# A four-layer trunk on one core: first gate tiles plain, operand sums of x moved, weight splits off GpSimd

## The chip, the cores and the metric

One core of one Trainium2 chip runs the whole program in one launch. The metric is the device time of one execution in microseconds (us), given as the median of several runs.

TensorE (PE in the profile) multiplies, VectorE (DVE), ScalarE (ACT) and GpSimd (POOL) do everything elementwise, and SyncE (SP) issues most DMAs. PEld is TensorE's weight load, listed apart from the matmuls.

## The reference, cut to what matters

The trunk has four residual layers over x, 512 tokens by 1024 features, in float32: pooling, gated convolution, latent attention, pooling. Each normalises x, multiplies by one input projection that yields the branch and a gate of width 2048, and ends in an output projection.

```
def rms_norm(x, g):  y = x * rsqrt(mean(x * x) + eps);  return y * g

def pool_mixer(xn, w_in, w_grp, scale, w_out):
    u, z = split(xn @ w_in, 2)                 # 2048 columns each
    for g, w in enumerate((2, 4, 8, 16)):      # groups of 512 columns
        pooled[g] = trailing_mean(u[g], w) - u[g]
        mixed[g] = pooled[g] @ w_grp[g]
    return (mixed * scale * silu(z)) @ w_out

def mla_mixer(...):                            # 16 heads
    q, k, v = low-rank latents @ up-projections;  p = softmax(q k^T + rotary part)
    return (p v * silu(z)) @ w_out
```

## The kernel before

**Precision.** Every operand of a matmul is split into a high part and the rest: ACT copies a tile to `fp32r` (h), DVE subtracts (l = value minus h). A product is then three matmuls: h by h, h by l, l by h (`mm3`, L256). The weights arrive in float32 and are split in the same way: `prepare_chunk` (L237) splits a chunk of 128x1024, ACT writing `wh` (L244) and DVE `wl` (L247). With `pool=True` both halves are done by POOL (L242, L247).

**Jobs.** The projections run as a stream of jobs (`Stream`, L184). One job is a plain tile (`Layer.tile`, L469): 24 matmuls 128x512 with one 512 KB chunk of weights; or a pair (`Layer.pair`, L484): two output tiles by seven half-width products (`seven`, L428), 84 matmuls of 256 columns. A pair needs weight blocks and their sums (`load_pair`, `prepare_pair`, L113 and L385: four loads from SP, an accumulating one from POOL, and on DVE the splits al, sl, cl, two sums, two tl) and needs the sums and differences of the halves of x (`XNorm.forms`, L350: per pair of x tiles four operations d at L362 to L365 on 128x256, two splits fh, fl). Its results E and O leave PSUM by two DVE operations (L458, L459).

**Order.** Each job has positions 0 to 7 (`now(k)`). The other engines' work is put on positions with `Steps.put`; what is put past 7 runs in later jobs. `Stream.step` (L213) loads the weights of the next two jobs, and puts the splitting of the next job's weights (`wh` on position 1, `wl` on 2) behind what already stands on the same position. Within the stream, TensorE, VectorE and ScalarE run strictly in the written order. GpSimd is not in that list. The attention heads (L1059 to L1085) are outside the stream, and there the framework's planner sets the order.

**The first layer.** Jobs in order: the first two u tiles with x still arriving (`first_two`), u02, u03, u10 to u13, the gate pairs z00 and z01, the mixes m00 and m01, the pairs z10 and z11, and so on (`ORDER`, L583). The normalising factor R comes from the statistics of x and is known after u11 (`at=(4, 6)`); until then six u tiles wait in PSUM. Then each gets (`post_u`, L595) a multiplication by R (L579, read from PSUM), adds with shifted copies on POOL (L608: one for group 0, two for group 1), a mean on DVE (L615, L616, L617), and a split (L620 on ACT, L623 on DVE); mean, high and low stand 12, 14 and 16 positions after the multiplication. The six start one position apart (`gap` 1). The forms of x for kk = 0 to 3 begin on positions 0, 8, 16 and 24 after `first_two`, one set in each of u02, u03, u10 and u11.

**Between layers.** `out_part` (L522) adds each output tile to x and puts the next layer's `xn.add(m)`, whose forms are delayed by `wait=8 * (KD - 2 - m + m // 2)`: set kk = 0 in the last job of the output projection, the others in the next layer's first three jobs. The convolution has four plain tiles before its first pair, the attention layer six.

**The attention heads.** Weight chunks are split by `wchunk(..., pool=True)` in `values`, `qrope` and `stage_a`; POOL also scales the softmax (L1021). From head 10, `split_y(nc.gpsimd)` takes the low part of two gated outputs per head (L1055). Transposes of p (L1034) wait for the scaling.

Of the kernel before, what the change touches and what calls it, by code (L numbers as in the profile page):

```python
# [9 lines left out]
F32 = mybir.dt.float32  # L10
# [54 lines left out]
def trunk_kernel(ctx: ExitStack, tc: tile.TileContext, a):  # L65
# [9 lines left out]
    def nm(s):  # L75
        cnt[0] += 1
        return f"{s}_{cnt[0]}"
# [86 lines left out]
    class Steps:  # L164
# [3 lines left out]
        def __init__(self, at=()):  # L168
            self.at = dict(at)

        def put(self, at, by=0):
            for pos, fns in at.items():
                self.at.setdefault(pos + by, []).extend(fns)

        def __call__(self, pos):
            while True:
# [7 lines left out]
    class Stream:  # L184
# [28 lines left out]
        def step(self):  # L213
            j = self.at
            self.at += 1
            self.load(j + 1)
            self.load(j + 2)
            now, self.later = self.later, Steps()
            now.put(self.prepare(j + 1), 2 if self.jobs[j][0] is PAIR and self.jobs[j + 1 :] and self.jobs[j + 1][0] is not PAIR else 0)
            self.jobs[j][2](self.ready.pop(j, None), now)  # L220
            now(7)
            left, self.later = self.later, Steps()
            self.later.put(now.at, -8)
            self.later.put(left.at)
# [297 lines left out]
    def out_part(stream, w, ys, hf, xn=None, also=(), scale=None):  # L522

        thens = []
        for m in range(KD):

            def then(o, m=m):
                if scale is not None:
                    t = ut("xs")
                    tmul(t, o, scale())  # L530
                    o = t
                nc.vector.tensor_tensor(out=xt[m], in0=o, in1=xt[m], op=ALU.add)
                if xn is not None:
                    stream.later.put(xn.add(m, wait=8 * (KD - 2 - m + m // 2)))
                if m < len(also):
                    also[m]()

            if m < 2:
                thens.append(then)
            else:  # L540
                stream.add(*half_job(w, ys, m, hf, lambda: ps("o"), 0, 8, then))
            if m == 1:

                open_ = []

# [12 lines left out]

                for q in range(2):
                    stream.add(CHUNK, w[q, hf], lambda wl, now, q=q: part(wl, now, q))  # L560
# [17 lines left out]
    def tmul(dst, src, R):  # L578
        nc.vector.tensor_tensor(out=dst, in0=src, in1=R, op=ALU.mult)  # L579
# [6 lines left out]
    def pool_layer(stream, j, xn, half, mid=None, at=(1, 3), pre=None):  # L586

        wu, wz, wg = a[f"pool_u{j}"], a[f"pool_z{j}"], a[f"pool_grp{j}"]
        ys = [[], []]
        ly = Layer(xn, at, 3 if pre is None else 1)  # L590
        u_, z_, m_ = {}, {}, {}
        for g, w in enumerate(WINDOWS):
            pooled, szs = [], []

            def post_u(t, sign, g=g, w=w, pooled=pooled):  # L595
                u = up.tile([P, S + PAD], F32, tag="u", name=nm("u"))
                h, l = ut("plh", F32R), ut("pll", F32R)
                pooled.append((h, l))
                sums = []

                def mul():
                    nc.gpsimd.memset(u[:, :PAD], 0.0)
                    tmul(u[:, PAD:], t, ly.R[sign])
                    cur, d = u, 1
                    while d < w:
                        nx = up.tile([P, S + PAD], F32, tag="u", name=nm("s"))
                        lo = 2 * d - 1
                        nc.gpsimd.tensor_tensor(out=nx[:, lo:], in0=cur[:, lo:], in1=cur[:, lo - d : S + PAD - d], op=ALU.add)  # L608
                        cur, d = nx, 2 * d
                    sums.append(cur)  # L610

                def mean():
                    cur, pd = sums[0], sums[0][:, PAD:]
                    hd = sp.tile([P, PAD], F32, tag="hd", name=nm("hd"))
                    nc.vector.tensor_tensor(out=hd, in0=cur[:, PAD : 2 * PAD], in1=con[:, C_INV + PAD * g : C_INV + PAD * (g + 1)], op=ALU.mult)  # L615
                    nc.vector.scalar_tensor_tensor(out=pd, in0=cur[:, PAD:], scalar=1.0 / w, in1=u[:, PAD:], op0=ALU.mult, op1=ALU.subtract)  # L616
                    nc.vector.tensor_tensor(out=pd[:, :PAD], in0=hd, in1=u[:, PAD : 2 * PAD], op=ALU.subtract)  # L617

                def high():
                    nc.scalar.activation(h, sums[0][:, PAD:], AF.Copy)  # L620

                def low():
                    nc.vector.tensor_tensor(out=l, in0=sums[0][:, PAD:], in1=f(h), op=ALU.subtract)  # L623

                return {0: [mul], 12: [mean], 14: [high], 16: [low]}

            def post_z(t, sign, szs=szs):
                def scale():
                    tmul(t, t, ly.R[sign])

                def gate():
                    nc.scalar.activation(t, t, AF.Silu)
                    szs.append(t)

                return {0: [scale], 3: [gate]}

# [25 lines left out]
            for i in range(4):  # L662
                u_[g, i] = lambda g=g, i=i, post_u=post_u: ly.tile(stream, wu[4 * g + i], post_u)
            for i in range(2):
                z_[g, i] = lambda g=g, i=i, post_z=post_z: ly.pair(stream, wz[2 * g + i], (post_z, post_z), mid and mid(g, i))
                m_[g, i] = lambda mix=mix, i=i: mix(i)
            if g == 0 and pre is not None:
                u_[0, 0] = lambda post_u=post_u: stream.add(None, None, lambda w, now: ly.done(stream, *[(post_u, t, 1) for t in pre()]))
# [116 lines left out]
    def mla_layer(stream, xn, begin, cos_sin, nxt):  # L785
# [159 lines left out]
        krh, krl = kr  # L945

        def values(g):
            wh, wl = wchunk(wv[g], pool=True)
            for tk in range(NT):
                pv = ps("pv")  # L950
                for k in range(2):
# [6 lines left out]
                vs[g, tk] = split(pv, "v")  # L958

        def qrope(g):  # L960
            wh, wl = wchunk(wq[8 + g], 768, pool=True)
            ab = []
            for e in range(2):
                pa = ps("pa")
# [19 lines left out]

        def stage_a(h):
            if h % 2 == 0:
                hold["q"] = wchunk(wq[h // 2], 768, pool=True)
            if h % 4 == 0:
                hold["k"] = wchunk(wk[h // 4], pool=True)
            pq = ps("pq")  # L990
            mtile(pq, *hold["q"], ql, kn=3, ktot=3, stride=2 * P, off=(h % 2) * P)
            q = split(pq, "q")
# [66 lines left out]
        for h in range(H):  # L1059
# [17 lines left out]
            extra(3)  # L1077
            if h >= SPLIT_Y_FROM:
                for _ in range(2):
                    split_y(nc.gpsimd)  # L1080
            if h + 1 == H:
                nxt.begin()
                nxt.step()
# [25 lines left out]
    def first_two():  # L1109
# [30 lines left out]
            s1.later.put({m: [lambda m=m: xn0.st.add(xt[m])]})  # L1140
        s1.later.put({10: [xn0.st.close]})
        for kk in range(KK):
            s1.later.put(xn0.forms(kk), 8 * kk)
        return pre

    pool_layer(s1, 0, xn0, half, at=(4, 6), pre=first_two)
# [136 lines left out]
def _layout(i):  # L1283
# [38 lines left out]
    }  # L1322
    for j in range(2):
        out[f"pool_u{j}"] = w_in(i["pool_w_in"][j][:, :DI])
        out[f"pool_z{j}"] = w_pair(i["pool_w_in"][j][:, DI:])
        out[f"pool_grp{j}"] = i["pool_w_grp"][j].reshape(4, 4, P, 2, 2 * P).transpose(0, 3, 2, 1, 4).reshape(4, 2, P, CH)
    w = i["mla_w_in"][0]
# [28 lines left out]
```

## Time and profile before

| | us |
|---|---|
| median of 3 runs (1519.23 to 1524.7) | 1521.63 |
| the profiled execution | 1516.26 |
| its span | 1514.4 |
| TensorE busy in the span | 1455.7 (96%) |
| VectorE busy | 1096.8 (72%) |
| ScalarE busy | 677.9 (45%) |
| GpSimd busy | 324.9 (21%) |

The profile takes one execution. Of the busy times only those near the whole span bound it on their own; an engine's wait is listed with what ended it. In the rows below, a duration includes the time in which an instruction is held up after it has started.

### The profile page before, as it was taken

Reading aid. Unit: us, or ns where it says so; the run is one execution under the profiler, and the core shown is the slowest. Engines: PE = TensorE matmul, PEld = TensorE weight load, DVE = VectorE, ACT = ScalarE, POOL = GpSimd, SP = SyncE. Lnnn points to the kernel's source line nnn. Section 1 sums busy time; section 2 is a strip of 40 time slices with the busy share of each in tenths; the row PEclk is TensorE's granted clock in tenths of the full one; section 3 lists DMA queues with packets and bytes.
Section 4 is the critical chain, followed back from the end, with each engine's and each line's share of the span. In section 5 each row is a group of like instructions: output and inputs, shape, how many; then the busy total and the mean of one; then the engine's idle time right before and its main releaser. Section 6 shows DMA issues by size and latency. Waiting matters only on the chain.

```text
span 1514.4 us, 22602 instructions
## 1 busy us (share of the span) xinstructions
PE 1455.7 (96%) x8632; PEld 1281.9 (85%) x8632; DVE 1096.8 (72%) x1757; ACT 677.9 (45%) x1170; POOL 324.9 (21%) x337
## 2 busy tenths in 40 slices
PE   9799999999999999999989998999999999999997
PEld 7698797887999899999869977888888798888886
DVE  7985557659989879998778867666655487755854
ACT  5353242445555335554455644444633354323333
POOL 2502206021000000000211014355501122310602
PEclk9899999999999999999999999999999999999999
DMA  6353354325676366665236641222122434333431
GB/s 218 89 136 119 88 149 98 126 84 121 180 194 174 126 148 182 173 188 174 84 90 170 169 130 37 69 70 84 43 84 84 111 107 110 129 101 114 123 112 56
DMA packets 66012, 183.30 MB, mean 121 GB/s; under 512 B 8176, under 2 KB 8176, under 8 KB 65904
## 3 DMA queue, kind: packets, MB, share of 16 engines
q1 hardware_dynamic: 57264, 151.97, 31.2%
q0 software_dynamic: 7776, 28.32, 11.4%
q10 hardware_dynamic: 864, 1.57, 0.3%
q8 instruction: 68, 1.11, 0.3%
q14 instruction: 40, 0.33, 0.1%
HBM read 175.27 MB, written 2.10 MB: 117 GB/s over the span
## 4 chain that ended last, share of the span: by engine, by line
PE 68%; DVE 16%; DMA 4%; issue 4%; ACT 4%; POOL 2%; SPq 0%; POOLq 0%; DVEq 0%; ACTq 0%
PE o L259 6%; PE o L257 6%; PE o L258 6%; PE bx L425 5%; PE bx L419 5%; PE bx L424 5%; PE bv L419 3%; PE bv L425 3%; PE bv L424 3%; PE pt L257 3%; PE pt L258 3%; PE pt L259 3%; DMA s<-in_conv_in 2%; DVE wl L247 2%; PE po L258 2%
## 5 line engine op out<-in xcount | busy, mean ns | idle before, releaser
L247 DVE TENSOR_TENSOR wl<-wr,wh 128x1024 fp32r<-128x1024 f32 (+1 forms) x120 | 154.2, 1286 | 52.5 <-ACT wh L244 52.4
L244 ACT ACTIVATE wh<-wr 128x1024 fp32r<-128x1024 f32 (+1 forms) x120 | 125.5, 1048 | 129.9 <-PE o L258 48.2
L259 PE MATMUL o<-yh,wl 128*128 128x512 f32 x384 | 151.6, 395 | 1.9 <-DVE wl L247 1.9
L258 PE MATMUL o<-yl,wh 128*128 128x512 f32 x384 | 151.2, 394 | 0.2 <-DVE yl L656 0.2
L257 PE MATMUL o<-yh,wh 128*128 128x512 f32 x384 | 151.3, 394 | 0.1
L259 PE MATMUL pt<-xh,wl 128*128 128x512 f32 x335 | 132.1, 395 | 4.1 <-DVE wl L247 4.1
L257 PE MATMUL pt<-xh,wh 128*128 128x512 f32 x335 | 132.8, 397 | 2.1 <-ACT xh L347 1.2
L258 PE MATMUL pt<-xl,wh 128*128 128x512 f32 x335 | 132.0, 394 | 0.6 <-DVE xl L348 0.6
L120 POOL DMA_DIRECT2D s<-in_conv_in x30 | 26.0, 868 | 324.4 <-DVE O L459 154.1
L439 ACT ACTIVATE kept<-bv 128x256 f32<-128x256 f32 x54 | 20.7, 384 | 163.5 <-PE bv L425 119.1
L395 DVE TENSOR_TENSOR sl<-s,sh 128x1024 fp32r<-128x1024 f32 x54 | 66.7, 1236 | 30.5 <-ACT sh L392 26.5
L259 PEld LDWEIGHTS o<-yh,wl 128*128 128x128 f32 x384 | 72.1, 188 | 19.5 <-DVE wl L247 2.8
L258 PEld LDWEIGHTS o<-yl,wh 128*128 128x128 f32 x384 | 72.1, 188 | 17.4 <-DVE yl L656 0.5
L257 PEld LDWEIGHTS o<-yh,wh 128*128 128x128 f32 x384 | 72.1, 188 | 16.9 <-ACT yh L653 0.5
L281 POOL TENSOR_TENSOR sq<-sq,sq 128x512 f32<-128x512 f32 x25 | 40.1, 1606 | 210.8 <-ACT sq L275 210.6
L608 POOL TENSOR_TENSOR s<-u 128x527 f32<-128x527 f32 x32 | 48.0, 1501 | 164.9 <-DVE u L579 135.2
L259 PEld LDWEIGHTS pt<-xh,wl 128*128 128x128 f32 x335 | 62.9, 188 | 20.4 <-DVE wl L247 6.1
L257 PEld LDWEIGHTS pt<-xh,wh 128*128 128x128 f32 x335 | 62.9, 188 | 17.5 <-ACT xh L347 2.1
L395 DVE TENSOR_TENSOR al<-wr,ah 128x1024 fp32r<-128x1024 f32 x54 | 66.5, 1232 | 14.5 <-ACT ah L392 12.4
L258 PEld LDWEIGHTS pt<-xl,wh 128*128 128x128 f32 x335 | 62.9, 188 | 15.6 <-DVE xl L348 1.5
L439 ACT ACTIVATE kept<-bx 128x512 f32<-128x512 f32 x108 | 53.0, 490 | 45.6 <-PE bx L425 45.6
L608 POOL TENSOR_TENSOR s<-s 128x525 f32<-128x525 f32 (+2 forms) x48 | 70.0, 1458 | 12.8 <-PE pm L258 9.6
(307 smaller groups left out, 4782.9 us busy)
## 6 DMA issues: line engine op xcount, KB each, us to landing
wr<-in_conv_in SPq DMA_DIRECT2D x34, 512.0 KB, 5.6
wr<-in_pool_out SPq DMA_DIRECT2D x32, 512.0 KB, 3.3
wr<-in_pool_u SPq DMA_DIRECT2D x30, 512.0 KB, 3.5
s<-in_conv_in SPq DMA_DIRECT2D x60, 256.0 KB, 4.5
s<-in_conv_in POOLq DMA_DIRECT2D x30, 512.0 KB, 6.2
wr<-in_pool_z SPq DMA_DIRECT2D x16, 512.0 KB, 4.3
s<-in_pool_z SPq DMA_DIRECT2D x32, 256.0 KB, 3.9
s<-in_pool_z POOLq DMA_DIRECT2D x16, 512.0 KB, 6.0
```

The costliest lines, as they stand in the source:

```text
L244: nc.scalar.activation(h, raw, AF.Copy)
L247: (nc.gpsimd if pool else nc.vector).tensor_tensor(out=l, in0=raw, in1=f(h), op=ALU.subtract)
L257: nc.tensor.matmul(out, ah, bh, start=first, stop=False)
L258: nc.tensor.matmul(out, ah, bl, start=False, stop=False)
L259: nc.tensor.matmul(out, al, bh, start=False, stop=last)
L281: eng.tensor_tensor(out=self.sum, in0=self.sum, in1=sq, op=ALU.add)
L395: return lambda: nc.vector.tensor_tensor(out=l, in0=t, in1=f(h), op=ALU.subtract)
L419: i = nc.tensor.matmul(out, wh[:, c], xh, start=begin and kk == 0, stop=False, skip_group_check=True)
L424: nc.tensor.matmul(out, wh[:, c], xl, start=False, stop=False, skip_group_check=True)
L425: nc.tensor.matmul(out, wl[:, c], xh, start=False, stop=end and kk == KK - 1, skip_group_check=True)
L439: nc.scalar.activation(dst, src, AF.Copy)
L608: nc.gpsimd.tensor_tensor(out=nx[:, lo:], in0=cur[:, lo:], in1=cur[:, lo - d : S + PAD - d], op=ALU.add)
```

## The change

The first layer's z00 and z01 become two plain tiles each, with their own copy of the weights (`pool_z00`), written to fresh tiles before the gate. The waiting u tiles start six positions apart, and the forms of x begin on positions 24, 40, 56 and 72. The forms after `out_part` come one job later. The weight splits of the next job are put ahead of what stands on the same position. The chunks in the attention heads are split by ACT and DVE, and `split_y` uses DVE. The adds of `post_u` are written as a list of steps on the same position.

```
-        def put(self, at, by=0):
+        def put(self, at, by=0, first=False):
             for pos, fns in at.items():
-                self.at.setdefault(pos + by, []).extend(fns)
+                l = self.at.setdefault(pos + by, [])
+                l[:] = [*fns, *l] if first else [*l, *fns]
...
-            now.put(self.prepare(j + 1), 2 if ... else 0)
+            now.put(self.prepare(j + 1), 2 if ... else 0, first=True)
...
-                    stream.later.put(xn.add(m, wait=8 * (KD - 2 - m + m // 2)))
+                    stream.later.put(xn.add(m, wait=8 * (KD - 1 - m + m // 2)))
...
-        ly = Layer(xn, at, 3 if pre is None else 1)
+        ly = Layer(xn, at, 3 if pre is None else 6)
...
+        def two_tiles(stream, src, posts, then):
+            for q in range(2):
+                ly.tile(stream, a["pool_z00"][len(zs)], posts[q], then if q else None)
+                zs.append(q)
...
-                return {0: [mul], 12: [mean], 14: [high], 16: [low]}
+                adds = [lambda q=q: add(2**q) for q in range(g + 1)]
+                return {0: [mul, *adds], 12: [mean], 14: [high], 16: [low]}
...
+                sz = ut("sz") if plain else t        # post_z, plain: g == 0 of the first layer
-                    tmul(t, t, ly.R[sign])
+                    tmul(sz, t, ly.R[sign])
...
-                z_[g, i] = lambda ...: ly.pair(stream, wz[2 * g + i], (post_z, post_z), ...)
+                z_[g, i] = lambda ...: (ly.pair if g or pre is None else two_tiles)(...)
...
-            wh, wl = wchunk(wv[g], pool=True)        # the same in qrope and stage_a
+            wh, wl = wchunk(wv[g])
...
-                    split_y(nc.gpsimd)
+                    split_y()
...
-            s1.later.put(xn0.forms(kk), 8 * kk)
+            s1.later.put(xn0.forms(kk), 24 + 16 * kk)
...
+            out["pool_z00"] = w_in(i["pool_w_in"][j][:, DI : DI + 4 * P])
```

## Rows read from the trace of the kernel before

**Rows 1.** The page's first part: busy time of an engine, its share of the span, its instructions.

```profile
PE 1455.7 (96%) x8632; PEld 1281.9 (85%) x8632; DVE 1096.8 (72%) x1757; ACT 677.9 (45%) x1170; POOL 324.9 (21%) x337
```

**Rows 2.** TensorE's waits over the whole span: tile and line that waited, what for, us in total, times, the longest.

```profile
PE bx L425 <- DVE tl L395: 8.4, 9, 2.9
PE pt L259 <- DVE wl L247: 4.1, 4, 1.7
PE pj L1034 <- POOL p L1021: 3.8, 4, 1.8
```

**Rows 3.** Stretches of the span: from and to in us, length, busy time of each engine (instructions), granted TensorE clock (1.00 is 2.4 GHz, 0.50 is 1.2 GHz), DMA share, GB/s. The first three are u12 with u13; z00; m00 with m01. Then z10 with z11, a stretch in the convolution's start, the attention heads, and two pieces within these.

```profile
43.00:54.30 11.30, 11.10 (x49) 8.72 (x48) 11.06 (x19) 5.57 (x8) 7.29 (x10) 1.00 0.56 136
54.30:78.20 23.90, 15.17 (x73) 14.27 (x73) 23.49 (x33) 9.07 (x16) 11.58 (x11) 0.64 0.29 78
89.40:100.50 11.10, 11.10 (x51) 9.04 (x50) 9.22 (x12) 5.55 (x8) 1.75 (x3) 1.00 0.62 144
100.50:120.40 19.90, 19.90 (x170) 19.90 (x169) 15.15 (x22) 10.54 (x18) 0.10 (x1) 1.00 0.56 167
340.00:350.00 10.00, 7.04 (x28) 4.79 (x28) 7.61 (x13) 4.42 (x8) 0.87 (x1) 1.00 0.26 56
893.00:1098.00 205.00, 191.81 (x1025) 163.85 (x1025) 131.29 (x343) 99.25 (x262) 96.98 (x107) 0.97 0.23 67
898.00:904.00 6.00, 6.00 (x16) 4.84 (x16) 0.35 (x1) 0.93 (x1) 1.18 (x2) 0.50 0.63 167
944.00:950.00 6.00, 5.98 (x24) 5.25 (x24) 1.76 (x5) 0.00 (x0) 0.00 (x0) 0.63 0.44 104
```

**Rows 4.** TensorE in order of time in the first layer: start, us, line, tile, in brackets the wait before it. The first row is u12's first matmul; then z00's first and its two long waits; m00's first; z10's first.

```profile
42.41 0.39 PE L257 MATMUL pt<-xh,wh 128*128 128x512 f32 x1
54.11 0.28 PE L419 MATMUL bx<-xh,ah 128*128 128x256 f32 x1
58.53 0.58 PE L425 MATMUL bx<-xh,al 128*128 128x256 f32 x1 [4.03 <-DVE al L395]
73.39 0.58 PE L425 MATMUL bx<-fh,tl 128*128 128x256 f32 x1 [2.89 <-DVE tl L395]
89.43 0.39 PE L257 MATMUL pm<-plh,wh 128*128 128x512 f32 x1
100.49 0.28 PE L419 MATMUL bx<-xh,ah 128*128 128x256 f32 x1
```

**Rows 5.** Groups of instructions between 43 and 100 us, shapes kept apart: count, busy us, mean ns, idle before.

```profile
L608 POOL TENSOR_TENSOR s<-u 128x527 f32<-128x527 f32 x8 | 10.9, 1363 | 10.3 <-DVE u L579 9.9
L608 POOL TENSOR_TENSOR s<-s 128x525 f32<-128x525 f32 x4 | 7.0, 1748 | 0.2
L616 DVE SCALAR_TENSOR_TENSOR s<-s,u 128x512 f32<-128x512 f32 x8 | 7.3, 907 | 0.3
L579 DVE TENSOR_TENSOR u<-pt,R 128x512 f32<-128x512 f32 x8 | 5.0, 681 | 0.0
L615 DVE TENSOR_TENSOR hd<-s,con 128x16 f32<-128x16 f32 x8 | 4.8, 599 | 0.0
L617 DVE TENSOR_TENSOR s<-hd,u 128x16 f32<-128x16 f32 x8 | 4.4, 547 | 0.3
L395 DVE TENSOR_TENSOR al<-wr,ah 128x1024 fp32r<-128x1024 f32 x3 | 3.7, 1219 | 0.3 <-ACT ah L392 0.3
```

**Rows 6.** VectorE, ScalarE and TensorE in order of time, single instructions: a form beside POOL's sums of squares and one without; R; a hd and a mean that stand alone.

```profile
18.98 1.52 DVE L362 SCALAR_TENSOR_TENSOR d<-x,par,g 128x256 f32<-128x256 f32 x1
30.60 0.48 DVE L362 SCALAR_TENSOR_TENSOR d<-x,par,g 128x256 f32<-128x256 f32 x1
...
45.09 0.58 ACT L321 ACTIVATE R<-pr 128x512 f32<-128x512 f32 x1
...
85.30 0.17 DVE L615 TENSOR_TENSOR hd<-s,con 128x16 f32<-128x16 f32 x1
85.50 0.69 DVE L616 SCALAR_TENSOR_TENSOR s<-s,u 128x512 f32<-128x512 f32 x1
```

**Rows 7.** The first tiles of the convolution (343 us) and of the attention layer (763 us) on TensorE, and the form on VectorE that stands ahead of the last tile of x there.

```profile
343.02 0.50 PE L259 MATMUL pt<-xh,wl 128*128 128x512 f32 x1 [1.72 <-DVE wl L247]
752.54 1.52 DVE L362 SCALAR_TENSOR_TENSOR d<-x,par,g 128x256 f32<-128x256 f32 x1
762.70 0.50 PE L259 MATMUL pt<-xh,wl 128*128 128x512 f32 x1 [1.73 <-DVE wl L247]
765.59 0.50 PE L290 MATMUL st<-ssh,ones 128*128 128x512 f32 x1 [1.00 <-ACT ssh L158]
```

**Rows 8.** The attention heads: two waits of TensorE, one VectorE operation between them, groups of POOL's splits between 893 and 1098 us, and a wait of POOL (us in total, times, the longest).

```profile
895.82 0.50 PE L259 MATMUL pk<-lnh,wl 128*128 128x512 f32 x1 [2.10 <-DVE wl L247]
932.39 2.33 DVE L975 TENSOR_TENSOR qr<-qr,sin 128x512 f32<-128x512 f32 x1
942.45 1.76 PE L1007 MATMUL s<-kh,qh 128*128 128x512 f32 x3 [4.86 <-ACT kh L158]
...
L247 POOL TENSOR_TENSOR wl<-wr,wh 128x768 fp32r<-128x768 f32 x10 | 19.1, 1913 | 0.8
L247 POOL TENSOR_TENSOR wl<-wr,wh 128x1024 fp32r<-128x1024 f32 x6 | 15.6, 2597 | 0.5
...
POOL wh L242 <- PE pq L258: 11.4, 4, 8.1
```

More of the change, by code (lines that the diff above doesn't have):

```diff
@@ L218, in step @@
             now, self.later = self.later, Steps()
-            now.put(self.prepare(j + 1), 2 if self.jobs[j][0] is PAIR and self.jobs[j + 1 :] and self.jobs[j + 1][0] is not PAIR else 0)
+            now.put(self.prepare(j + 1), 2 if self.jobs[j][0] is PAIR and self.jobs[j + 1 :] and self.jobs[j + 1][0] is not PAIR else 0, first=True)
             self.jobs[j][2](self.ready.pop(j, None), now)
@@ L589, in pool_layer @@
         ys = [[], []]
-        ly = Layer(xn, at, 3 if pre is None else 1)
+        ly = Layer(xn, at, 3 if pre is None else 6)
         u_, z_, m_ = {}, {}, {}
+        def two_tiles(stream, src, posts, then):
+            for q in range(2):
+                ly.tile(stream, a["pool_z00"][len(zs)], posts[q], then if q else None)
+                zs.append(q)
+        zs = []
         for g, w in enumerate(WINDOWS):
@@ L603, in mul, with add @@
                     tmul(u[:, PAD:], t, ly.R[sign])
[L604 to L610, printed above, removed]
+                    sums.append(u)
+                def add(d):
+                    cur, nx = sums[0], up.tile([P, S + PAD], F32, tag="u", name=nm("s"))
+                    lo = 2 * d - 1
+                    nc.gpsimd.tensor_tensor(out=nx[:, lo:], in0=cur[:, lo:], in1=cur[:, lo - d : S + PAD - d], op=ALU.add)
+                    sums[0] = nx
                 def mean():
@@ L623, in low, with post_z @@
                     nc.vector.tensor_tensor(out=l, in0=sums[0][:, PAD:], in1=f(h), op=ALU.subtract)
-                return {0: [mul], 12: [mean], 14: [high], 16: [low]}
-            def post_z(t, sign, szs=szs):
+                adds = [lambda q=q: add(2**q) for q in range(g + 1)]
+                return {0: [mul, *adds], 12: [mean], 14: [high], 16: [low]}
+            def post_z(t, sign, szs=szs, plain=g == 0 and pre is not None):
+                sz = ut("sz") if plain else t
                 def scale():
-                    tmul(t, t, ly.R[sign])
+                    tmul(sz, t, ly.R[sign])
                 def gate():
-                    nc.scalar.activation(t, t, AF.Silu)
-                    szs.append(t)
+                    nc.scalar.activation(sz, sz, AF.Silu)
+                    szs.append(sz)
                 return {0: [scale], 3: [gate]}
@@ L664, in pool_layer @@
             for i in range(2):
-                z_[g, i] = lambda g=g, i=i, post_z=post_z: ly.pair(stream, wz[2 * g + i], (post_z, post_z), mid and mid(g, i))
+                z_[g, i] = lambda g=g, i=i, post_z=post_z: (ly.pair if g or pre is None else two_tiles)(stream, wz[2 * g + i], (post_z, post_z), mid and mid(g, i))
                 m_[g, i] = lambda mix=mix, i=i: mix(i)
@@ L960, in qrope @@
         def qrope(g):
-            wh, wl = wchunk(wq[8 + g], 768, pool=True)
+            wh, wl = wchunk(wq[8 + g], 768)
             ab = []
@@ L986, in stage_a @@
             if h % 2 == 0:
-                hold["q"] = wchunk(wq[h // 2], 768, pool=True)
+                hold["q"] = wchunk(wq[h // 2], 768)
             if h % 4 == 0:
-                hold["k"] = wchunk(wk[h // 4], pool=True)
+                hold["k"] = wchunk(wk[h // 4])
             pq = ps("pq")
@@ L1324, in _layout @@
         out[f"pool_u{j}"] = w_in(i["pool_w_in"][j][:, :DI])
+        if j == 0:
+            out["pool_z00"] = w_in(i["pool_w_in"][j][:, DI : DI + 4 * P])
         out[f"pool_z{j}"] = w_pair(i["pool_w_in"][j][:, DI:])
```

## The prediction

> **What bounds the kernel now.** I read the page's busy times first. TensorE is busy for 1455.7 of 1514.4 us [rows 1], so 58.7 us of waiting is the first thing a change can win, and the second is time at the lower clock. The whole-span list of waits then says what TensorE waits for: nearly always VectorE's low parts of weights, and in the heads GpSimd's scaling (3.8) [rows 2]. The stretches show where. Between 54.3 and 78.2 us TensorE is busy for 15.17 of 23.90 us at a granted clock of 0.64, while VectorE is busy for 23.49 [rows 3]: the first gate pair is VectorE's stage. The order of time shows it as two waits, 4.03 us for al and 2.89 us for tl, and z00 with z01 takes 54.11 to 89.43, 35.3 us [rows 4], though two undisturbed pairs take 19.9 [rows 3]. The attention heads hold 13.2 us of TensorE's idleness (205.0 less 191.81) [rows 3].
>
> The sum is made on the profiled execution: 1516.26 us, 1.86 outside its span. It is 5.4 below the median 1521.63; I subtract the gain from the median.
>
> **1. The first layer.** *TensorE's side.* A 24-matmul job takes 5.55 us (11.10 for m00 and m01), a pair 9.95 (19.90 for two) [rows 3]. Four plain tiles for two pairs cost 22.2 against 19.9, so 2.3 us more of work. From u12's first matmul to z10's first, the floor becomes 6 x 5.55 + 11.1 = 44.4 us; it took 100.49 - 42.41 = 58.1 [rows 4]. If only TensorE counted, 13.7 us would go, and about 1 more because the forms no longer stand in front of u12's and u13's weights.
>
> *VectorE's side.* I count its instructions from the first multiplication by R to z10's al. Terms by duration: 0.68 for a 128x512 operation, 1.22 for 128x1024, a mean 0.17 + 0.69 + 0.17 = 1.03 where nothing disturbs it, a set of forms 4 x 0.48 + 2 x 0.68 = 3.3 [rows 5, 6]. Common to both kernels: 8 multiplications 5.4, 8 means 8.2, 8 low parts 5.4, 4 gate scalings 2.7, 6 operations of the mixes 4.1, z10's al 1.2; together 27.0. Before adds three wl (3.7), two pair preparations of 2 x 1.22 + 5 x 0.68 = 5.8 (11.7) and four E and O (2.7): 45.1. After adds seven wl (8.5) and three sets of forms (9.8): 45.3. **VectorE's own work in this stretch does not shrink**: what the pairs gave up, the later forms take.
>
> *The hold-ups.* Beside POOL's twelve adds, hd takes 0.599 instead of 0.17, the mean 0.907 instead of 0.69, its correction 0.547 instead of about 0.17; times eight that is 8.1 us [rows 5, 6]. Multiplications from PSUM show none. The adds stay twelve (17.9 us on POOL [rows 5]) and are only spread, so I keep 8: at least 4 (half of them fall beside multiplications or idle time), at most 12 (each add costs one us). As a test, before gives 45.1 + 8.1 = 53.2 from R's end at 45.67 [rows 6] to z10, and 54.8 passed.
>
> *The start.* R came 3.3 us after u12's first matmul, because VectorE did forms ahead of the statistics' reduction and the first of them stood 1.52 beside POOL instead of 0.48 [rows 6]. Two sets leave the jobs ahead of that reduction; I put R's end at 42.4, between 41.8 and 45.7. So z10 begins at 42.4 + 45.3 + 8 = 95.7 instead of 100.5: **5 us gained**. Upper end 14.5 (TensorE's floor); lower end -4 (R no earlier, 12 of hold-ups, 105). What is late next is wl of z01's tiles: VectorE's load from z00's second tile to z01's first exceeds the 5.55 us of a job by some 3, behind which the scale, the forms and the next wl queue. The plain loads from SP are 512 KB each and replace the pairs' four loads and POOL's accumulating one; they go ahead by two jobs and I cost them at nothing. If SP held them for a free buffer, one job's 5.55 would show.
>
> The 4.03 us wait was followed by a granted clock of 0.64 in its stretch, while 1.72 + 1.00 + 0.23 in the convolution's start left 1.00 [rows 3, 4, 7]. My sum takes no loss of clock: VectorE, late anyway, hides a slow TensorE between two waits. The Trainium skill (TensorE: Matmul & The Clock Gate, section "Why this matters for your kernels") says that an idle gap between bursts of matmuls returns the array to the lower clock, which speaks against plain tiles that wait for wl. The trace agrees for the long wait and not for the broken one; the case has its own place among the rivals.
>
> **2. Between the layers.** The first wl of the convolution and of the attention layer are waited for 1.72 and 1.73, the statistics 1.00 [rows 7]. In the second place the forms (1.52 for one beside POOL) ran in the last output job, ahead of the last tile of x. One job later they let that tile pass, and the weights stand first. In the attention layer six plain tiles follow, with room for the forms: 3 us gained (2.7 in the two rows, the rest small waits there), between 1 and 4. In the convolution only four follow, and the fourth set now falls on the same job as the first pair's al: the 2.7 won come back as a late tl, so **0, between -3 and 2**. Weights first elsewhere swaps operations of under 1.3 us that rarely share a position: 0, between -1 and 1.
>
> **3. The heads.** POOL's sixteen low parts take 19.1 + 15.6 us, three of them in a row around 932 to 942 us, where a VectorE operation of 0.68 takes 2.33 and TensorE waits 4.86 [rows 8]. Afterwards the clock is at 0.63 for 6 us, 2.2 lost; the 2.10 wait at 895 is followed by 6 us at 0.50, 3.0 lost [rows 3, 8]. With pj's 3.8 [rows 2] this is 16 us, all that the change could win here. I take 3.5 of 5.1 at the start, 5 of 7.1 around 942 and 1.5 of pj's 3.8 (POOL keeps the scalings): 10. Against it come sixteen high parts on ACT and on VectorE sixteen low parts of at most 1.22 with twelve of 0.68, 27.7 us into 73.7 idle ones; ACT has 105.8 idle [rows 3]. Each can stand ahead of an exponential or a maximum. The trace shows none there: between 0 and 16 x 2 x 1.22 = 39 us. I take 3, nearer to 0, since less than 40% of the idle time is used and the splits wait only for loads and buffers. **7 us gained**, between -23 and 16.
>
> Sum: 5 + 3 + 0 + 7 = 15. 1521.6 - 15 = **1506.6 us**.
>
> **The rivals.**
> *VectorE gives nothing back.* The first layer stays at VectorE's pace, since its work there is equal (45.1 and 45.3), and the heads swap a hold-up by POOL for a queue of their own. Only the 3 us between the layers remain: 1518.6. For it: VectorE full in the first pair. Against: the earlier R, and 16 us in the heads.
> *Slower: ScalarE and VectorE stand where POOL stood.* POOL's wh waits for TensorE to free a weight buffer, 11.4 us in four waits, the longest 8.1 [rows 8], and nobody minds. On ACT the same wait holds up the exponentials queued behind it, then POOL's scaling, then TensorE's transposes. Full price: 11.4, and 3.0 for the clock after the longest, 14.4 lost in place of 7 won: 1521.6 + 14.4 - 8 = 1528. It decides from some 8 us of such waits (the other gains) upward. For it: in-order engines. Against: the planner sees these waits when it orders the heads, and can put the wh behind them.
> *The clock falls at each late wl.* Two waits in z01's tiles each leave 6 us at half clock, 3.0 lost as at 898 us [rows 3]; TensorE then sets the pace, the first layer gives 5 - 6 = -1, and 9 remain: 1512.6. For it: 0.64 in the first pair. Against: the broken wait. This is what the page's rule would do here.
> *Everything opens.* The spread adds meet only free moments, the first layer reaches TensorE's floor (14.5), the heads win 13: 1521.6 - 30.5 = 1491. Against: twelve adds are still there.
>
> **The numbers.** Forecast 0.53, VectorE-bound 0.17, clock 0.10, slower 0.12, all open 0.08. The range 1493 to 1523 leaves out the last two; within it the lower end is 28.6 won (first layer 12, between layers 4, heads 12.6), the upper end 1.4 lost. A difference of 0.3% (4.6 us) is what a measurement can tell from none. Faster by more: nearly all of the forecast (0.50) and of the clock case (0.09), the open case, a quarter of the VectorE-bound one (0.04): 0.71. Within: the rest of these three but 0.01, 0.03 + 0.01 + 0.12 = 0.16. Slower: 0.12 + 0.01 = 0.13.
>
> **What would show it.** Right: z10's first matmul near 95 us and waits for wl in z01's tiles; hold-ups of means still there; no waits for the first wl of the attention layer; no 4.9 us wait near 940, clock 1.00 behind it; the convolution's first pair late by a tl. Wrong: z10 at 86 or after 100; ACT idle on a buffer with an exponential queued behind; new waits of s or pj above 7 us in all. The forecast fails if the heads lose, or if the first layer's waits only change their name.

## The result, and the profile after

The kernel after takes 1502.99 us (median of 4 runs, 1499.11 to 1504.05) beside 1520.43 for the kernel before (4 runs). The ratio is 0.988, with a 95% interval of 0.9847 to 0.9914: 18 us, between 13 and 23. The forecast was 15 us. The profiled execution took 1502.28 us, its span is 1500.5. A second set of runs of the same kernel, further down, gives 0.9891 (0.987 to 0.9913).

The page's first part for the kernel after, to be read beside [rows 1]:

```profile
PE 1451.2 (97%) x8560; PEld 1273.3 (85%) x8560; DVE 1086.7 (72%) x1771; ACT 686.9 (46%) x1174; POOL 258.3 (17%) x291
```

TensorE's busy time falls by 4.5 us, the span by 13.9: most of it is waiting that has gone. GpSimd has lost 67 us of work, and VectorE is not busier, though it took over the sixteen low parts. TensorE's waits in the whole span of the kernel after (in total, times, longest), those that answer to [rows 2] and [rows 8]:

```profile
PE bx L426 <- DVE tl L396: 6.4, 10, 1.9
...
PE pt L260 <- DVE wl L248: 4.0, 3, 2.4
...
PE s L1018 <- ACT kh L158: 3.2, 3, 2.0
...
PE pj L1045 <- POOL p L1032: 2.4, 1, 2.4
...
PE pk L260 <- DVE wl L248: 0.2, 1, 0.2
```

The total of pt's waits for wl is as before, 4.0 beside 4.1, but it has moved. In the kernel before 3.45 of it stood at the starts of two layers [rows 7]; now 3.2 of it stands in the first layer's new plain tiles. The stretches of the kernel after (columns as in [rows 3]): u12 and u13; z00's two tiles; z01's two; m00 and m01; and two pieces within the attention heads.

```profile
42.00:53.30 11.30, 11.30 (x51) 9.13 (x50) 8.01 (x11) 4.39 (x7) 5.31 (x7) 1.00 0.27 94
53.30:64.60 11.30, 11.22 (x49) 8.73 (x47) 11.13 (x17) 3.06 (x5) 6.60 (x7) 1.00 0.14 46
64.60:83.80 19.20, 14.44 (x49) 10.74 (x50) 18.14 (x32) 9.41 (x15) 6.98 (x6) 0.82 0.19 55
83.80:95.90 12.10, 11.39 (x49) 8.78 (x48) 10.07 (x18) 6.50 (x9) 0.68 (x1) 1.00 0.60 131
930.00:936.00 6.00, 5.26 (x21) 4.04 (x22) 3.84 (x8) 1.98 (x6) 0.00 (x0) 0.72 0.52 144
942.00:950.00 8.00, 6.12 (x31) 5.69 (x32) 5.74 (x19) 4.42 (x13) 1.82 (x4) 0.79 0.14 55
```

The first layer has one bad stretch left, 64.6 to 83.8, with VectorE busy for 18.14 of 19.20 us. TensorE in order of time shows what it waits for in z01's tiles, and z10's first matmul (the last row):

```profile
65.79 0.50 PE L258 MATMUL pt<-xh,wh 128*128 128x512 f32 x1 [1.27 <-ACT wh L245]
68.95 0.80 PE L260 MATMUL pt<-xh,wl 128*128 128x512 f32 x1 [2.42 <-DVE wl L248]
...
77.01 0.50 PE L258 MATMUL pt<-xh,wh 128*128 128x512 f32 x1 [0.37 <-ACT wh L245]
78.51 0.50 PE L260 MATMUL pt<-xh,wl 128*128 128x512 f32 x1 [0.77 <-DVE wl L248]
...
95.90 0.28 PE L420 MATMUL bx<-xh,ah 128*128 128x256 f32 x1
```

z10 begins at 95.90, where 95.7 was forecast and 100.49 stood before [rows 4].

In the experiments a *milestone* is the start of a job's first matmul, and a step is by how much a stretch between two milestones got shorter against the profiled execution of the kernel before. In the kernel after the steps are: up to z10 4.6; the convolution up to its first pair 3.5; the convolution behind that -9.1; the attention layer up to its first pair 3.1; from there to the first scores 5.3; the heads 4.7; the last layer up to its last mixes 2.8. One execution does not fix such a step: in the five profiles of kernels with this same first layer z10 begins between 95.38 and 98.15.

### The profile page after: what moved, and what is told of

It is laid out like the page before. It is cut to its first block, busy times and chain, and to the rows that moved or that the text cites. A ratio compares the mean times of both kernels' runs of the same rounds, so it can differ in the third digit from the quotient of the medians.

```text
span 1500.5 us, 22412 instructions
## 1 busy us (share of the span) xinstructions
PE 1451.2 (97%) x8560; PEld 1273.3 (85%) x8560; DVE 1086.7 (72%) x1771; ACT 686.9 (46%) x1174; POOL 258.3 (17%) x291
## 5 line engine op out<-in xcount | busy, mean ns | idle before, releaser
L248 DVE TENSOR_TENSOR wl<-wr,wh 128x1024 fp32r<-128x1024 f32 (+1 forms) x140 | 173.1, 1236 | 55.9 <-ACT wh L245 54.7
L245 ACT ACTIVATE wh<-wr 128x1024 fp32r<-128x1024 f32 (+1 forms) x140 | 144.4, 1034 | 147.7 <-PE o L259 47.7
L260 PE MATMUL pt<-xh,wl 128*128 128x512 f32 x367 | 145.3, 397 | 4.0 <-DVE wl L248 4.0
L258 PE MATMUL pt<-xh,wh 128*128 128x512 f32 x367 | 146.2, 398 | 2.7 <-ACT wh L245 2.5
L259 PE MATMUL pt<-xl,wh 128*128 128x512 f32 x367 | 145.2, 396 | 0.6 <-DVE xl L349 0.6
L260 PEld LDWEIGHTS pt<-xh,wl 128*128 128x128 f32 x367 | 69.5, 189 | 21.6 <-DVE wl L248 5.3
L259 PEld LDWEIGHTS o<-yl,wh 128*128 128x128 f32 x384 | 72.1, 188 | 17.2 <-DVE yl L667 0.5
L258 PEld LDWEIGHTS pt<-xh,wh 128*128 128x128 f32 x367 | 69.5, 189 | 19.9 <-ACT wh L245 3.8
L259 PEld LDWEIGHTS pt<-xl,wh 128*128 128x128 f32 x367 | 69.5, 189 | 16.5 <-DVE xl L349 1.0
L393 ACT ACTIVATE sh<-s 128x1024 fp32r<-128x1024 f32 x52 | 54.9, 1055 | 35.1 <-DMA s<-in_conv_in 17.8
```

The source lines that it names most:

```text
L245: nc.scalar.activation(h, raw, AF.Copy)
L248: (nc.gpsimd if pool else nc.vector).tensor_tensor(out=l, in0=raw, in1=f(h), op=ALU.subtract)
L258: nc.tensor.matmul(out, ah, bh, start=first, stop=False)
L259: nc.tensor.matmul(out, ah, bl, start=False, stop=False)
L260: nc.tensor.matmul(out, al, bh, start=False, stop=last)
L393: return lambda: nc.scalar.activation(h, t, AF.Copy)
```

## The experiments

Times are compared with runs of the kernel before on the same chip. A gain in us is one less the ratio, times the median before; its ends are those of the interval.

### One part of the change by itself

**The heads alone**, in the kernel before:

```
-            wh, wl = wchunk(wv[g], pool=True)      # also in qrope, stage_a
+            wh, wl = wchunk(wv[g])
-                    split_y(nc.gpsimd)
+                    split_y()
```

> The kernel before with the heads' sixteen weight chunks and the twelve late low parts moved off GpSimd, nothing else changed. Hold-up theory: the heads give what they gave in the whole change, 9 to 11 us from the start of the heads to their end, so 1509 to 1512 us, with no wait above 2.5 us near 940. Rival (the heads only gain because the stream in front of them delivers sooner): under 4 us, 1516 to 1520.

Measured: ratio 0.995 (0.9931 to 0.997), 7.6 us gained (4.6 to 10.5). The step of the heads is 6.4. The chunks and `split_y` moved together; no run takes them apart.

**The first layer alone**: the kernel after without weights first, without the later forms and with the heads of before.

```
-            now.put(self.prepare(j + 1), ..., first=True)
+            now.put(self.prepare(j + 1), ...)
-                    stream.later.put(xn.add(m, wait=8 * (KD - 1 - m + m // 2)))
+                    stream.later.put(xn.add(m, wait=8 * (KD - 2 - m + m // 2)))
...
```

> Only the first layer's part: gate tiles plain, six positions between the waiting tiles, sums of x on 24, 40, 56, 72; weights stay behind in their positions, the forms between layers and the heads as before. VectorE-bound theory: z10's first matmul at 95 to 97 us against 100.5, total 3 to 5 us under the kernel before, 1515 to 1517. Rival (the late low part of the weights is what the ahead-order cures): z10 at 98 or later, total within 2 us of before.

Measured: ratio 1.0003 (0.9983 to 1.0024), no gain. In its trace z10 begins 2.5 us sooner, and 1.6 of that is gone by the end of the layer.

**All but weights first**: the kernel after with only the first line of the diff above.

> The changed kernel with the next job's weight splits put behind, as before, instead of ahead of what shares their position. If the order within a position matters little, as I forecast: within 2 us of the changed kernel, 1501 to 1505. Rival: it is the order that costs the convolution its new waits (6.4 us lost between its first pair and its end) or that wins the 3.5 us of the last layer; then these differ and the total moves by 3 to 6 us either way.

Measured: 0.9947 (0.9924 to 0.997), 8.0 us gained. Some 9 of the change's 17 to 18 us are lost with that one argument. The heads alone would account for what is left.

**The forms one job sooner again**: the kernel after with only the second.

> The changed kernel with the forms of the next layer one job sooner again, as before. Theory: the attention layer's start loses 3 us (waits of 1.7 and 1.0 return), the convolution's start changes by less than 1.5, total 1505 to 1507. Rival: the later forms cost the convolution more than they win (its new late tl and its later waits come from them): total 1499 to 1502.

Measured: 0.9897 (0.9859 to 0.9934), not to be told from the kernel after. In the trace the step up to the attention layer's first pair falls from 3.1 to 1.4, and the one in the convolution from 3.5 to -0.2, so the later forms do move both pairs, but the timed runs are too coarse to show it.

### Weights first

**Weights first alone**, in the kernel before:

```
-            now.put(self.prepare(j + 1), ...)
+            now.put(self.prepare(j + 1), ..., first=True)
```

> The kernel before with one edit: the next job's weight splits stand ahead of what shares their position. Theory from the runs so far (behind instead of ahead cost the changed kernel 8 us, and the waits of 2.7 for kept in the last layer, 1.7 for the first wl of two layers, are gone wherever they stand ahead): 5 to 8 us faster than before, 1510 to 1513, those three waits gone. Rival (the order pays only together with the later forms and the plain tiles): within 2 us of before.

Measured: 0.9937 (0.9921 to 0.9953), 9.6 us gained (7.1 to 12.0), where the forecast had it at 0, between -1 and 1, everywhere but in the first layer and at the starts of the next two. By its trace, whose execution was the fastest of the ten, 2.8 us lie up to z10, 1.4 at the convolution's start, 3.4 ahead of the heads, 1.4 in them and 3.3 in the last layer. To find the jobs that gain, it was split in two:

```
-            now.put(self.prepare(j + 1), ...)
+            now.put(self.prepare(j + 1), ..., first=... self.jobs[j + 1][0] is PAIR)      # pairs
+            now.put(self.prepare(j + 1), ..., first=... self.jobs[j + 1][0] is not PAIR)  # plain tiles
```

> The kernel before, with the weights put first only where the next job is a pair. 'Weights first' as a whole took 9.5 us (1509.8). Theory P (the gain is made by the pairs' preparations: fewer waits for tl and for the second half of a result, as the 2.69 us before the pair at 1275 us): the median comes 5 to 9 us under the kernel before, the wait of 2.69 near 1275 us falls under 0.5, and the waits of 1.72 and 1.73 us for the first wl of the convolution and of the attention layer stay. Theory C (the gain is made by the plain jobs' chunks at the starts of the layers): within 3 us of the kernel before, and the waits at the starts stay.

> The kernel before, with the weights put first only where the next job is a plain tile. Theory C (the plain jobs' chunks make the gain): the two waits of 1.7 us for wl at the starts of the convolution and of the attention layer fall under 0.5 and the median comes 5 to 9 us under the kernel before. Theory P (the pairs make it): those waits fall too, but the time stays within 4 us of the kernel before, and the wait of 2.69 us near 1275 us stays. If the two parts are simply added, this run and the one with pairs alone give 9.5 us together.

Measured: before pairs alone 0.9961 (0.9939 to 0.9982), 5.9 us; before plain tiles alone 0.9978 (0.9959 to 0.9998), 3.3 us. Together 9.2, so the parts add up. By the conditions put on record both runs come out for theory P: some two thirds come from the pairs (between 2.7 and 9.3 us, the plain tiles between 0.3 and 6.2).

The pairs' share can be read in the last layer. First the kernel before, its stretch from 1275 us on (columns as in [rows 3]):

```profile
1275.00:1280.00 5.00, 5.00 (x30) 5.00 (x31) 2.96 (x5) 2.58 (x4) 0.00 (x0) 0.66 0.46 129
```

The same kernel in order of time: GpSimd's issue of a load, a subtraction on VectorE, two adds of GpSimd, the operation of VectorE that needs them, and the wait of TensorE that follows.

```profile
1261.92 0.88 POOL L120 DMA_DIRECT2D s<-in_pool_z  x1 [7.50 <-DVE wr L398]
1262.04 2.42 DVE L395 TENSOR_TENSOR tl<-wr,th 128x512 fp32r<-128x512 f32 x1 [0.70 <-ACT th L392]
1262.53 1.37 POOL L608 TENSOR_TENSOR s<-u 128x527 f32<-128x527 f32 x1
1263.97 1.40 POOL L608 TENSOR_TENSOR s<-s 128x525 f32<-128x525 f32 x1
...
1265.40 0.18 DVE L615 TENSOR_TENSOR hd<-s,con 128x16 f32<-128x16 f32 x1 [0.95 <-POOL s L608]
...
1274.85 0.38 PE L419 MATMUL bv<-xh,ch 128*128 128x256 f32 x1 [2.69 <-ACT kept L439]
```

And with weights first before pairs, in order of time: the same operations of the same job, and TensorE's one wait for such a copy in this layer's mixes:

```profile
1255.91 1.88 POOL L609 TENSOR_TENSOR s<-u 128x527 f32<-128x527 f32 x1 [3.90 <-DVE u L580]
...
1259.03 0.69 DVE L396 TENSOR_TENSOR tl<-wr,th 128x512 fp32r<-128x512 f32 x1 [0.70 <-ACT th L393]
1259.75 0.87 POOL L120 DMA_DIRECT2D s<-in_pool_z  x1 [1.97 <-ACT th L393]
1260.36 1.36 POOL L609 TENSOR_TENSOR s<-s 128x525 f32<-128x525 f32 x1
...
1261.76 0.18 DVE L616 TENSOR_TENSOR hd<-s,con 128x16 f32<-128x16 f32 x1 [2.03 <-POOL u L603]
...
1282.74 0.39 PE L420 MATMUL bv<-xh,ch 128*128 128x256 f32 x1 [0.33 <-ACT kept L440]
```

With weights first the pair's preparation stands 3.0 us sooner (tl at 1259.03 instead of 1262.04); 0.6 of it is an earlier start of the layer. The same subtraction takes 2.42 us where it meets GpSimd's adds and 0.69 where it falls between them, but its length is not what the rest waits for: in both kernels VectorE then stands until GpSimd's adds are done, and hd begins 3.6 us sooner. In the kernel before, both adds stand behind GpSimd's issue of a load, which waits for the preparation; with weights first one add has gone ahead of the issue, and the issue itself comes sooner. What VectorE and ScalarE have queued behind hd moves with it, and the wait for the copy `kept` goes from 2.69 us to nothing at this job and 0.33 a job later. This is read from the two traces; no run holds GpSimd's order fixed.

Behind the wait of before the granted clock stood at 0.66 for 5 us, 1.7 us lost. 2.7 less 0.3 plus 1.7 make 4.1 us, and the step of this stretch is 3.8. Ahead of the heads (800 to 893 us) the same edit shortens a wait for tl at 821 us from 1.60 to 1.00 and all waits together from 3.6 to 2.5, and the clock, which stood at 0.95 and 0.87 between 813 and 833 us (1.8 us lost), stays at 1.00: 2.9 of a step of 3.4. The plain tiles' share lies at the starts of the convolution and of the attention layer, 1.4 each: the waits for wl of 1.72 and 1.73 [rows 7] are 0 and 0.22, but the wait for the statistics right behind grows from 1.00 to 1.61. In the kernel with the whole edit the second of these steps is -0.2: TensorE's waits there are the same, but its clock then stands at 0.83 for 10 us (1.7 lost).

### GpSimd beside VectorE

**Half of the heads' splits on GpSimd.** In the first kernel GpSimd makes the high part of the chunks, in the second the low part; the rest is the kernel after.

```
-            wh, wl = wchunk(wv[g])                          # also in qrope, stage_a
+            wh, wl = wchunk(wv[g], pool=True)
-            (nc.gpsimd if pool else nc.vector).tensor_tensor(out=l, ...)   # first kernel
+            nc.vector.tensor_tensor(out=l, ...)
-            if pool:                                               # second kernel
+            if False:
```

> The changed kernel with the heads' chunks split half and half: the high parts (one input) on GpSimd, the low parts on VectorE. If GpSimd's two-input low parts were what held up VectorE, the heads keep their gain: start to end of heads within 1.5 us of the changed kernel, total 1501 to 1505. Rival (GpSimd's queue, in which the softmax scalings wait behind splits, is what cost the heads): half of the gain goes, 1505 to 1508.

> The other half: high parts on ScalarE, low parts on GpSimd. Hold-up theory: the three long operations of 2.3 to 2.9 us in the rotary part and a wait near 4 us around 935 return, the heads lose 4 to 7 us, total 1507 to 1510. Rival (ScalarE's and VectorE's added work is what limits the heads now): 1501 to 1504.

Beside them, on the same chip, the kernel after once more:

> The changed kernel once more, beside the others on the same chip: 1500 to 1505. Late landings of the convolution's weights fall on other pairs than in the first profile, if they are chance; the same pairs (421 and 484 us), if the change moved a load.

Measured: 0.9897 (0.9881 to 0.9914) with the high part on GpSimd, 0.9897 (0.9865 to 0.9929) with the low part, and 0.9891 (0.987 to 0.9913) for the kernel after. The three can't be told apart by their times. The traces can: with the high part on GpSimd the heads step is 2.0, with the low part 4.6, in the kernel after 4.7 and 6.1. Why so little is left in the first is seen at the wait that was 4.86 before [rows 8]. With the high part on GpSimd, VectorE, GpSimd, ScalarE and TensorE in order of time:

```profile
926.02 1.06 POOL L243 TENSOR_SCALAR wh<-wr 128x1024 fp32r<-128x1024 f32 x1 [3.09 <-PE pq L259]
926.14 1.47 DVE L985 TENSOR_TENSOR t<-qr,cos 128x512 f32<-128x512 f32 x1
927.41 0.91 POOL L243 TENSOR_SCALAR wh<-wr 128x768 fp32r<-128x768 f32 x1 [0.33 <-PE pk L259]
927.54 1.31 DVE L161 TENSOR_TENSOR qal<-t,qah 128x512 fp32r<-128x512 f32 x1
...
929.91 0.68 DVE L987 TENSOR_TENSOR t<-t,qr 128x512 f32<-128x512 f32 x1
...
930.68 0.63 ACT L158 ACTIVATE qbh<-t 128x512 fp32r<-128x512 f32 x1 [4.33 <-DVE t L987]
931.70 0.59 ACT L158 ACTIVATE kh<-pk 128x512 fp32r<-128x512 f32 x1
932.34 1.10 PE L1018 MATMUL s<-kh,qh 128*128 128x512 f32 x3 [3.69 <-ACT kh L158]
```

In the kernel after, ScalarE makes both wh, and the same chain is shorter:

```profile
926.06 1.06 ACT L245 ACTIVATE wh<-wr 128x1024 fp32r<-128x1024 f32 x1 [2.65 <-PE pq L259]
926.35 0.69 DVE L985 TENSOR_TENSOR t<-qr,cos 128x512 f32<-128x512 f32 x1
...
928.29 0.68 DVE L987 TENSOR_TENSOR t<-t,qr 128x512 f32<-128x512 f32 x1
...
928.89 0.68 DVE L161 TENSOR_TENSOR qal<-t,qah 128x512 fp32r<-128x512 f32 x1
...
930.73 1.56 PE L1018 MATMUL s<-kh,qh 128*128 128x512 f32 x3 [1.99 <-ACT kh L158]
```

Two copies on GpSimd stretch the two VectorE operations beside them by 0.78 and 0.63, 1.4 us in all. They stand ahead of the sum that qbh needs (L987), kh stands behind qbh in ScalarE's queue, and so the wait is 3.69 instead of 1.99. The order differs too: here qal stands ahead of that sum, in the kernel after behind it. The second kernel missed its forecast of 4 to 7 us lost. Its hold-ups did come back: VectorE's operations of 128x512 in the heads exceed 0.69 by 7.9 us in all (10.8 before, 0.1 after, 2.4 in the first kernel), yet its step is that of the kernel after, and the wait at that place is 1.87. So the hold-ups by themselves do not set what the heads take; it depends on where they fall, and the planner chose another order in each kernel. What share of the heads' gain each kind of split has stays open.

**No adds beside the first layer's stream.** The kernel after, with GpSimd's adds left out for groups 0 and 1, so their trailing sums are not computed:

```
-                adds = [lambda q=q: add(2**q) for q in range(g + 1)]
+                adds = [lambda q=q: add(2**q) for q in range(0 if pre is not None and g < 2 else g + 1)]
```

> The kernel after, with GpSimd's adds of the first layer left out for groups 0 and 1 (these groups' trailing sums are not computed). Hold-up theory (the twelve adds cost VectorE some 8 us there): a mean of 512 columns falls back to 0.69 and its first column block to 0.17, the waits for wl of z01's first tile vanish, and z10 begins at 88 to 92 in place of 95.9. Rival, VectorE's own work of 45 us sets the pace: z10 stays within 1.5 us of 95.9, though the single operations become shorter.

Measured: one execution of 1490.38 us, z10 at 88.91, 7.0 sooner than in the kernel after. The waits in z01's tiles are 0.92 and 0.59 in place of 4.83. VectorE's groups between 42 and 98 us (columns as in [rows 5]) in the kernel after:

```profile
L248 DVE TENSOR_TENSOR wl<-wr,wh 128x1024 fp32r<-128x1024 f32 x7 | 9.2, 1312 | 0.9 <-ACT wh L245 0.9
L631 DVE TENSOR_TENSOR pll<-s,plh 128x512 fp32r<-128x512 f32 x8 | 6.3, 791 | 0.8 <-ACT plh L628 0.8
L624 DVE SCALAR_TENSOR_TENSOR s<-s,u 128x512 f32<-128x512 f32 x8 | 5.5, 692 | 0.3
...
L363 DVE SCALAR_TENSOR_TENSOR d<-x,par,g 128x256 f32<-128x256 f32 x3 | 3.0, 1015 | 0.0
L625 DVE TENSOR_TENSOR s<-hd,u 128x16 f32<-128x16 f32 x8 | 2.9, 362 | 0.3
```

The same groups without the adds:

```profile
L248 DVE TENSOR_TENSOR wl<-wr,wh 128x1024 fp32r<-128x1024 f32 x7 | 8.5, 1215 | 0.9 <-ACT wh L245 0.9
L624 DVE SCALAR_TENSOR_TENSOR u<-u 128x512 f32<-128x512 f32 x8 | 5.5, 692 | 0.3
...
L631 DVE TENSOR_TENSOR pll<-u,plh 128x512 fp32r<-128x512 f32 x8 | 5.5, 684 | 0.7 <-ACT plh L628 0.7
...
L363 DVE SCALAR_TENSOR_TENSOR d<-x,par,g 128x256 f32<-128x256 f32 x3 | 1.4, 477 | 0.0
...
L625 DVE TENSOR_TENSOR u<-hd,u 128x16 f32<-128x16 f32 x8 | 1.4, 175 | 0.3
```

The differences of the means times their counts: wl 0.7, pll 0.9, the forms 1.6 (L363) and 0.8 (L364: three, 744 and 476), the correction (L625) 1.5, hd 0.8 (eight, 273 and 168), and fl 0.9 (six, 830 and 686); 7.2 us in all. z10 moves by 7.0, and the stretch from R's end to it from 53.0 to 45.9. The hold-ups in the kernel after thus cost what they last, as they would where VectorE sets the pace. The multiplications by R, one of whose inputs lies in PSUM, take 0.684 with the adds and 0.685 without. The rule of the Trainium skill (SBUF — State Buffer, section "Who interferes with whom") is that a VectorE instruction with two inputs in SBUF contends with a GpSimd instruction that reads SBUF, and that one with at most one SBUF input, outside its modes that use two ports, does not. Both halves agree with these rows.

### A version that might have been better

**The forms on other positions**, in the kernel after:

```
-            s1.later.put(xn0.forms(kk), 24 + 16 * kk)
+            s1.later.put(xn0.forms(kk), (24, 32, 40, 72)[kk])
```

> The kernel after, with the first layer's sets of forms on positions 24, 32, 40 and 72 in place of 24, 40, 56 and 72: the second and third set go into u12 and u13, where VectorE is idle for 3.3 of 11.3 us, and leave z00's second tile and z01's first. If the two waits of z01's first tile (1.27 for wh, 2.42 for wl) are made by the load on VectorE at that place, they shrink by 2 us or more together, z10 begins at 92 to 94 in place of 95.9, and the median comes 1 to 3 us under the kernel after (ratio to before 0.987 to 0.988). Rival, VectorE's work is the same wherever it stands and the wait only moves: z10 within 1 us of 95.9 and the ratio at 0.989 to 0.991.

Measured: 0.9902 (0.9881 to 0.9922), no better than the kernel after. z10 stands at 94.86, and 0.4 of the 1.0 us is R, which came that much sooner in this execution; the rest is about as much as the same code differs by. The waits on the way are 6.1 us in all beside 5.5: they moved into z00's second tile. The rival holds by its time.

## Why the prediction was right, and where it was not

The time and the sign came out, but two terms of the sum were wrong in opposite directions, so that the sum came so near is in part luck.

**The heads.** The forecast's 7 us are 7.6 in the kernel with the heads alone. The pieces are not those that were priced. Of the 5.1 at the start nearly all came (a wait of 0.18, clock 1.00 behind it) instead of 3.5. Of the 7.1 around 942 only 3.4 did instead of 5: 1.99 of waiting is left, and the clock of 0.72 over 6 us still costs 1.7. Of pj's 3.8 nothing came in this execution: one wait of 2.39, and a clock of 0.79 over 8 us behind it (in the second profile of the kernel after 0.8 of waits are left). Of the 3 for new waits 1.7 came: TensorE's waits for kl grew from 1.6 to 3.3. In all that is 6 to 7 again. The slower rival's mechanism exists too. The list of ScalarE's waits in the heads of the kernel after (in total, times, longest):

```profile
ACT wh L245 <- PE pq L259: 8.9, 5, 2.6
...
ACT wh L245 <- PE pa L259: 3.8, 3, 1.3
...
ACT wh L245 <- PE pv L967: 1.7, 3, 0.6
```

Two of the waits for pq, 1.7 us, belong to chunks of the stream, which ScalarE split before as well. That leaves 12.7 us of ScalarE standing before a weight buffer of the heads, where GpSimd stood 16.8 for the same three tiles (11.4 of it for pq [rows 8]), and more than the 8 from which that rival was to decide. It did not decide, since the waits fall where little is queued. Behind the wh at 926.06 above, which waits 2.65, stands qah; behind each of the others stands the copy of the very product that the wh waits for.

**The first layer.** z10 at 95.90 is the forecast's 95.7, and its parts came too: R's end at 42.91 (42.4 was forecast), from there 53.0 us (45.3 + 8 were), hold-ups of 7.2 where 8 was taken. They sit on the forms, the corrections and the low parts, while a mean takes 0.692 as it does alone. In the five profiles with this first layer R ends between 42.36 and 44.62, but from there to z10 it is 53.0 to 53.5 us in each: VectorE's sum holds, and that R came so near to 42.4 is in part luck.

What failed is whose gain it is. The step ascribed all 5 us to the earlier R and the plain tiles. With the forms moved, R ends at 43.0 in the mean of nine profiles, and at 45.7 in the five with the old places, so that part came. But the stretch behind R gets no shorter by the plain tiles: 55.4 and 54.9 us without weights first, 54.8 and 55.3 in the old first layer (kernel before, heads alone). Weights first shortens it, to 53.4 in the old first layer and to 53.0 to 53.5 in the new. Neither half of that edit does as much (54.1 for the pairs, 55.2 for the plain tiles), and the timed run of the first layer alone shows no gain. The clock did fall in z01's stretch, to 0.82, and z10 was no later than VectorE's sum: VectorE hid it. The rule that the prediction weighed (the Trainium skill, TensorE: Matmul & The Clock Gate, section "Why this matters for your kernels") speaks of longer gaps than the 2.42 us here; the clock fell all the same, but that this would cost time did not come true.

**Between the layers.** The attention layer gives 3.1 where 3 was forecast, half of it by the later forms. The convolution's pair begins 3.5 sooner and then waits for the late tl that was forecast, but for 1.00 us only; with 1.04 for al and 0.29 for `kept`, 2.3 us of waits follow in place of none, so about 1 us stays in this execution; by the means further down nothing does, as forecast.

**The step that failed** reads "Weights first elsewhere swaps operations of under 1.3 us that rarely share a position: 0, between -1 and 1". The edit measured 9.6 alone, and by its trace 6.6 us lie in two places of that "elsewhere", ahead of the heads and in the last layer. Two things were left out. The order on a position also decides when GpSimd's issues and adds come, and what waits for them: in the last layer hd came 3.6 us sooner. And a wait of 1.6 to 2.7 us can be followed by a clock of 0.66 to 0.95, which cost 1.7 to 1.8 more. Both were in the prediction's own rows, at other places. Nor is it rare that operations share a position: a pair's preparation stands on six of them.

**How the sum stands.** Weights first (9.6) and the heads (7.6) alone make 17.2 of the 16.6 to 18.2 measured. By the traces the earlier R adds 2 to 3 us in the first layer on top of weights first, and the later forms some 2 at each of two layers' starts, before what the convolution loses again; the timed runs are too coarse to show that.

**A loss that was mostly chance.** From the start of its first pair on, the convolution is 9.1 us longer in the profiled execution after; 2.3 of that are the first pair's waits. ScalarE waits there for a load; from the list of its waits between 350 and 712 us (in total, times, longest) in the kernel after:

```profile
ACT sh L393 <- DMA s<-in_conv_in: 17.8, 7, 4.8
```

In the kernel before:

```profile
ACT sh L392 <- DMA s<-in_conv_in: 3.6, 4, 1.9
```

And in the kernel with the heads alone, whose convolution is that of before:

```profile
ACT sh L392 <- DMA s<-in_conv_in: 10.4, 6, 3.6
```

With unchanged instructions that stretch was 6.4 us longer in the last of these than in the one before it. In the second profile of the kernel after it was 3.4 longer, with 11.5 us of such waits. The profiled execution of before has the least of all profiles taken, so the comparison of two profiles charged the change for luck. Not all of it: in the seven profiles with the later forms the stretch is 3.4 to 9.1 us longer than in that one (6.7 in the mean), in the seven others -0.4 to 6.5 (3.1), so some 3.6 go with the later forms, about what they gain up to the first pair. Nor do the waits for the loads order the lengths: 15.5 us of them stand beside 4.2 more (weights first before pairs), 10.5 beside 8.7 (forms on other positions). Why the loads land late in one execution and not in another stays open.

## What to carry to other kernels

Before an edit that only reorders work is priced at nothing, list what runs on GpSimd beside each place: an operation of VectorE costs by its neighbour as well as by its size. When VectorE sets the pace, take GpSimd's operations out one group at a time; what the others lose in duration is what the stage gains. Where VectorE does not set the pace, 7.9 us of hold-ups cost nothing that could be measured (the heads with the low part on GpSimd). And before a step between two milestones is given to a part of the change, split it at the event that releases the stage (here R's end): in five executions of the same first layer z10 moved by 2.8 us, the stretch behind R by 0.5.

## What was not expected

- A copy on GpSimd holds VectorE up as an add does: 1.47 and 1.31 us beside two copies, 0.69 and 0.68 without.
- Waits of like length leave different clocks: 1.60 us at 821 us in the kernel before was followed by 0.95 and 0.87, and 1.53 us at 856 us in the kernel with weights first before pairs by 1.00. At the start of the attention layer the same five waits (0.2 to 0.3, and one of 1.61) were followed by 1.00 with weights first before plain tiles and by 0.83 with weights first everywhere.
- The loads of the convolution made ScalarE wait between 3.6 and 17.8 us in the profiled executions of kernels that compute the same there.
